# Hybrid stream step: the last unit's ScalarE stores go to SP, a head's keys are loaded and split apart from its queries, and one normalization is read four ticks later

## The chip, the cores and the metric

The kernel runs on one core of a Trainium2 chip. The metric is the time of one execution on the device in microseconds. An execution was recorded by the hardware profiler as well; its trace is what the text below quotes.

## The reference, cut to what matters

One layer handles 512 frames of a new stream (the prompt) and 64 frames of a running one (the samples), which has 512 cached frames:

```python
hn = rmsnorm(x, g_norm1);  proj = hn @ w_in          # 576 x 2048 @ 2048 x 6144
q, k, v, gb, gc, hc = split(proj)                    # 8 heads x 128; 3 x 1024 channels
q = rmsnorm(q, g_q);  k = rmsnorm(k, g_k)            # per head and frame
# stick-breaking attention, strictly causal: z = q k / sqrt(128)
# w[t,s] = sigmoid(z[t,s]) * prod over s<j<t of (1 - sigmoid(z[t,j]));  o_attn = w @ v
o_conv = gb * causal_conv3(gc * hc)
x = x + concat(rmsnorm(o_attn), rmsnorm(o_conv)) @ w_out
h2 = rmsnorm(x, g_norm2)
x = x + (silu(h2 @ w_gate) * (h2 @ w_up)) @ w_down   # 2048 -> 5632 -> 2048
```

The outputs are the new x of both streams, the new keys and values, and the convolution's states.

## The kernel before, in words

Frames lie in the columns, 576 of them in two halves of 288 (`HALVES`), the first 512 the prompt's. Products are exact to float32: each operand is split into a rounded high part and a low part (`split`, L228 the cast on ScalarE, L229 the difference on VectorE), and the products high x high, low x high and high x low are added. The large projections run as units of seven products each (`run`, line 405 holds their matmuls), whose weights and frames are prepared ahead (`prepare`).

**The order of the work.** TensorE's order is the order in which the code is written. Work that has to stand between other work is written as generators of a `Pipeline`: a `yield n` puts the rest n ticks later, and a tick is, in the output projection, three matmuls of 288 columns (`product`, L224). ScalarE, VectorE, GpSimd and SP are ordered by a scheduler until the last phase, the down projection; there all four follow the code as well. `tc.issue_after(x)` keeps what is issued inside it behind instruction x.

**Normalization.** When a half of a head's queries or keys is done, `a_done` scales it (L899), squares it, casts the squares on ScalarE (L904) and takes the low part on VectorE (L905). `normed` (L844) waits 20 ticks and then sums high and low part over the channels with two matmuls (`channel_sums`, L283 and L284) on TensorE.

**Attention.** The output projection of the convolution's half (`out_proj`, `pjo`) fills TensorE while the eight heads go by, one every 29 ticks (`PERIOD`). `attend(h)` writes one head: the scores of the key blocks 2 and 3, 1, and 0 (`scores`, L1173 and L1176), their softplus, the scores of the samples' queries against their 64 new keys and the cached ones (`zs`, L1204) and their softplus, cumulated over blocks into `sp`. Eleven ticks later come the sums over keys that the product over j needs, block by block: block 2, four ticks, block 1, four ticks, block 0. `weights(b)` masks a block (L1229), takes its exponential (L1231) and splits it into `ph` and `pl`. Then the output `po` is summed: L1280 and L1283. Between, `sample_weights` adds the sums of `sp` to the samples' scores (L1219 to L1222, from `sph` and `spl`).

The queries and keys of the next head come from DRAM: `load_qk` (L1033) loads all 576 columns of both into `qf` and `kf`, behind the scores of the samples, which read both. `split_qk` splits their first 512 columns into `qh`, `ql`, `kh`, `kl` behind `weights(2)`; the samples' sums are split into `sph`, `spl` behind `weights(1)`. The next head's first scores read all four parts.

**The end.** The last unit of the down projection finishes four blocks of the output. All others are transposed by VectorE in pieces and stored by SP with six small DMAs each (`store_blocks`, L1613 and L1615), for a block nine and then five ticks behind its sum. The four of the last unit are transposed by TensorE (`store_y`, L1644), copied by ScalarE (L1647 and L1653) and stored row-wise: for the first half of the frames one DMA of SP (L1656) and GpSimd's, for the second half one of SP (L1635), then one of 96 rows (prompt) and one of 32 rows (samples) on ScalarE (`put`, L1635 and L1637), and GpSimd's.

Every DMA that SP or ScalarE issues adds to one of eight counters, DMAHW0 to DMAHW7, when it has landed. The counters are dealt out in turn to the DMAs of both engines together, in the order of the program, and a DMA is issued only when the one before it on its counter has landed.

Of the kernel before, what the change touches and what calls it, by code (L numbers as in the profile page):

```python
# [10 lines left out]
F32 = mybir.dt.float32  # L11
F32R = mybir.dt.float32r
AF = mybir.ActivationFunctionType
# [3 lines left out]
P = 128  # L17
TP = 512
TS = 64
T = TP + TS  # L20
# [5 lines left out]
NH = 8  # L26
# [32 lines left out]
NA = len(HEADS_A)  # L59
# [43 lines left out]
def tile_hybrid_stream_step(  # L103
# [6 lines left out]
    nc = tc.nc  # L110
    mm = nc.tensor.matmul
# [23 lines left out]
    qk_dram = tc.dram_tile([NH, 2, P, T], F32, name="qk_dram")  # L135
# [20 lines left out]
    NU = len(gu)  # L156
# [70 lines left out]
    def split(hi, lo, src, lo_eng=None):  # L227
        cast = nc.scalar.copy(out=hi, in_=src)  # L228
        (lo_eng or nc.vector).tensor_tensor(out=lo, in0=src, in1=hi.bitcast(F32), op=ALU.subtract)  # L229
        return cast.ins  # L230
# [611 lines left out]
        return ((a, min(b, TP), 0),) + (((TP, b, 2),) if b > TP else ())  # L842

    def normed(n, h, c, a, b, s2, E):  # L844
        yield 12 if n == -2 else 20
        ms = ss = channel_sums(s2[:, 0], s2[:, 1], a, b, "ss")
        yt = hl_tile("yt")
        y, t = yt[:, :HALF], yt[:, HALF:]
        nc.scalar.activation(out=ms, in_=ss, func=AF.Identity, scale=1.0 / P, bias=epsc)
        nc.scalar.activation(out=y, in_=ms, func=AF.Ln)  # L850
        nc.scalar.activation(out=y, in_=y, func=AF.Exp, scale=-0.5)
        nc.scalar.activation(out=t, in_=y, func=AF.Square)
        nc.vector.scalar_tensor_tensor(out=t, in0=t, scalar=-0.5, in1=ms, op0=ALU.mult, op1=ALU.mult)
        nc.vector.scalar_tensor_tensor(out=t, in0=t, scalar=1.5, in1=y, op0=ALU.add, op1=ALU.mult)
        nc.vector.scalar_tensor_tensor(out=E[:, a:b], in0=E[:, a:b], scalar=col("gk") if c else gqs, in1=t,
                                       op0=ALU.mult, op1=ALU.mult)
        seen[n, c] = seen.get((n, c), 0) + 1
        if seen[n, c] == 2:
            nc.sync.dma_start(out=qk_dram[h, c], in_=E)
            if c:  # L860
                pipe.spawn((last_tokens if n == -2 else tokens)(E, kp[:, h, :], ks[:, h, :], None, 11 if n == -2 else 20))
# [152 lines left out]
    free.clear()  # L1014
    lpool.release()
    bpool = tc.alloc_tile_pool(name="bpool", bufs=1, reuse_waits="tile", side="left")
    qf, kf = (bpool.tile([P, T], F32, name=name) for name in ("qf", "kf"))
    qh, ql, kh, kl = (bpool.tile([P, TP], F32R, name=name) for name in ("qh", "ql", "kh", "kl"))
    cK = bpool.tile([P, 4, P], F32, name="cK")
    ws = bpool.tile([P, 320], F32, name="ws")  # L1020
# [10 lines left out]
    vz = bpool.tile([P, 2, P], F32R, name="vz")  # L1031

    def load_qk(h):  # L1033
        nc.sync.dma_start(out=qf, in_=qk_dram[h, 0])
        nc.sync.dma_start(out=kf, in_=qk_dram[h, 1])

    def split_qk():
        split(qh, ql, qf[:, :TP])
        split(kh, kl, kf[:, :TP])

    def load_cached_keys(h):
        nc.sync.dma_start(out=cK, in_=ck[:, h, :].rearrange("(i p) d -> p i d", p=P))
# [5 lines left out]
        nc.sync.dma_start(out=cV, in_=cv[:, h, :].rearrange("(i p) d -> p i d", p=P))  # L1048

    load_qk(0)  # L1050
    split_qk()
    load_cached_keys(0)
    fetch_v(0)
# [76 lines left out]
    def softplus(dst, ps, scratch):  # L1130
        nc.scalar.activation(out=scratch, in_=ps, func=AF.Abs)
        nc.scalar.activation(out=scratch, in_=scratch, func=AF.Exp, scale=-1.0)
        nc.scalar.activation(out=scratch, in_=scratch, func=AF.Ln, bias=1.0)
        nc.vector.scalar_tensor_tensor(out=dst, in0=ps, scalar=0.0, in1=scratch, op0=ALU.max, op1=ALU.add)

    kw = dict(start=False, skip_group_check=True)
    bt = {}
# [27 lines left out]
    def attend(h):  # L1165
# [12 lines left out]
        for b in (2, 1, 0):  # L1178
# [15 lines left out]
            if b == 1:  # L1194
                nc.gpsimd.tensor_tensor(out=pb[1][:, P:], in0=pb[1][:, P:], in1=pb[2], op=ALU.add)
                split(s0h, s0l, pb[1])
            yield 3 if b else 1
            if h == 0 and b == 1:
                keys_cached(0)

        zs = misc("zs")
        for n, b in enumerate((4, 3, 2, 1, 0)):
            lk = kf[:, T - P : T] if b == 4 else kcT[:, b * P : (b + 1) * P]
            mm(zs[:, b * TS : (b + 1) * TS], lk, qf[:, TP:T], start=(n == 0), stop=False, skip_group_check=True)  # L1204
        if h + 1 < NH:
            load_qk(h + 1)
        softplus(sp[:, :320], zs[:, :320], sp[:, :320])
        nc.gpsimd.tensor_tensor(out=sp[:, 256:320], in0=sp[:, 256:320], in1=s01, op=ALU.mult)
        sums = sp[:, 320:]
        nc.gpsimd.tensor_copy(sums[:, 192:256], sp[:, 256:320])  # L1210
        for b in (2, 1, 0):
            nc.gpsimd.tensor_tensor(out=sums[:, b * TS : (b + 1) * TS], in0=sums[:, (b + 1) * TS : (b + 2) * TS],
                                    in1=sp[:, (b + 1) * TS : (b + 2) * TS], op=ALU.add)
        yield 8
        if h == 0:
            split_v()
# [23 lines left out]
        mm(zb[2], trir, ph[2], stop=False, **kw)  # L1240
        mm(zb[2], trir, pl[2], stop=True, **kw)
        behind = weights(2)
        if h + 1 < NH:
            with tc.issue_after(behind):
                split_qk()
        yield 4
        mm(zb[1], trir, ph[1], stop=False, **kw)
        mm(zb[1], trir, pl[1], stop=False, **kw)
        mm(zb[1][:, P:], neg1r, s1h, stop=False, **kw)
        mm(zb[1][:, P:], neg1r, s1l, stop=True, **kw)  # L1250
        behind = weights(1)
        with tc.issue_after(behind):
            split(sph, spl, sp)
        yield 4
        mm(zb[0], trir, ph[0], stop=False, **kw)
        mm(zb[0], trir, pl[0], stop=False, **kw)
# [365 lines left out]
    def store_y(n, c, i):  # L1622
# [16 lines left out]
        def work():  # L1639
# [15 lines left out]
            if i == 0:  # L1655
                nc.sync.dma_start(out=yp[: 2 * P, cs].rearrange("(i p) c -> p i c", p=P), in_=ob)  # L1656
            else:
                put(f0, ob[:, 0, :])
                put(f0 + P, ob[:, 1, :], nc.scalar if n == NU - 1 else nc.sync)
            put(f0 + 2 * P, obs, nc.gpsimd if n == NU - 1 else nc.sync)  # L1660

        pipe.spawn(work())
# [82 lines left out]
```

## Time and profile before

| | us |
|---|---|
| median of 3 runs | 2339.37 (2337.11 to 2339.61) |
| the profiled execution | 2339.12 |
| its span, first to last instruction | 2337.4 |
| TensorE busy (matmuls) | 2316.1 |
| VectorE, ScalarE, GpSimd busy | 1954.1, 1221.6, 300.6 |

The 1.7 us between the profiled time and the span lie around the recorded instructions. Rows of a timeline give the start in us from the span's start, the duration, the engine (a name ending in q is its queue, where DMAs are issued and semaphores awaited), the line, the operation, output and input, and in brackets the idle time ahead with what ended it. TensorE's matmuls overlap: when nothing is awaited the next one starts before the last has ended, so the distance of two starts is the price of one. Rows of waits give the sum, the times and the longest.

### The profile page before, as it was taken

How to read it: one execution, taken by the hardware profiler on the slowest of the kernel's cores; microseconds unless marked ns; L12 is line 12 of the kernel's file. 1: busy time of each engine (PE TensorE's matmuls, PEld its weight loads, DVE VectorE, ACT ScalarE, POOL GpSimd, SP SyncE). 2: the span in 40 equal slices, each digit the busy share in tenths (PEclk: the TensorE clock that was granted, in tenths of full speed). 3: DMA queues.
4: the chain of work that ended last, by engine and by line, in shares of the span. 5: the costliest groups of instructions: out<-in, count | busy, mean ns of one | idle time of the engine just before them, and what ended most of it. 6: DMA issues, size and time to landing. Idle time of an engine off the chain costs nothing.

```text
span 2337.4 us, 43553 instructions
## 1 busy us (share of the span) xinstructions
PE 2316.1 (99%) x17432; PEld 2306.9 (99%) x17432; DVE 1954.1 (84%) x2871; ACT 1221.6 (52%) x2170; POOL 300.6 (13%) x374
## 2 busy tenths in 40 slices
PE   9999999999999999999999999999999999999997
PEld 9999999999999999999999999999999999999997
DVE  8889989897777898888888888888888778887896
ACT  8556656456877654444444444444444444444443
POOL 0211121110332320000000000000000002431222
PEclk9999999999999999999999999999999999999999
DMA  8434343546743454543444444444444936875653
GB/s 271 139 113 129 91 142 110 142 134 206 197 137 118 163 190 126 159 152 121 154 142 136 154 129 149 143 139 150 130 148 140 361 115 225 227 217 188 208 133 80
DMA packets 533771, 368.58 MB, mean 158 GB/s; under 512 B 70278, under 2 KB 518016, under 8 KB 533568
## 3 DMA queue, kind: packets, MB, share of 16 engines
q1 hardware_dynamic: 526752, 356.32, 48.7%
q0 software_dynamic: 6384, 9.21, 2.2%
q8 instruction: 136, 2.23, 0.4%
q14 instruction: 67, 0.55, 0.1%
q10 hardware_dynamic: 432, 0.27, 0.0%
HBM read 285.52 MB, written 80.23 MB: 156 GB/s over the span
## 4 chain that ended last, share of the span: by engine, by line
PE 92%; DVE 3%; ACT 3%; DMA 1%; issue 1%; POOL 0%; SPq 0%; POOLq 0%; DVEq 0%; ACTq 0%
PE psy L405 45%; PE psw L405 23%; PE psx L405 11%; PE pjo L224 6%; PE pj L691 1%; PE pjz L691 1%; DVE whl L229 1%; PE psv L405 1%; PE pjm L691 1%; DMA raw_a<-in_w_down_dram 0%; ACT ph L228 0%; PE psx L556 0%; ACT whi L176 0%; DMA raw_b<-in_w_down_dram 0%; PE z L1176 0%
## 5 line engine op out<-in xcount | busy, mean ns | idle before, releaser
L229 DVE TENSOR_TENSOR whl<-raw_a,whl 128x1024 fp32r<-128x1024 f32 (+4 forms) x384 | 432.2, 1126 | 54.8 <-ACT whl L228 53.4
L405 PE MATMUL psy<-t,whl 128*128 128x288 f32 x3000 | 447.0, 294 | 0.0
L228 ACT CAST whl<-raw_a 128x1024 fp32r<-128x1024 f32 (+4 forms) x384 | 360.1, 939 | 141.5 <-PE psx L405 46.7
L405 PE MATMUL psy<-h_s,whl 128*128 128x288 f32 x2766 | 416.5, 294 | 0.6 <-ACT part L428 0.6
L405 PEld LDWEIGHTS psy<-t,whl 128*128 128x128 f32 x3000 | 414.3, 188 | 0.0
L405 PE MATMUL psw<-t,whl 128*128 128x288 f32 x2688 | 388.9, 294 | 0.0
L405 PEld LDWEIGHTS psy<-h_s,whl 128*128 128x128 f32 x2766 | 383.1, 188 | 0.9 <-ACT part L428 0.8
L405 PEld LDWEIGHTS psw<-t,whl 128*128 128x128 f32 x2688 | 366.8, 188 | 0.0
L228 ACT CAST whl<-raw_b 128x1024 fp32r<-128x1024 f32 (+5 forms) x234 | 211.3, 905 | 208.1 <-issue 71.6
L229 DVE TENSOR_TENSOR whl<-raw_b,whl 128x1024 fp32r<-128x1024 f32 (+5 forms) x234 | 254.7, 1089 | 74.0 <-ACT whl L228 72.6
L428 ACT COPY part<-psy 128x288 f32<-128x288 f32 x309 | 123.1, 399 | 343.3 <-PE psy L405 340.9
L405 PE MATMUL psx<-h_s,whl 128*128 128x288 f32 x1164 | 170.2, 294 | 0.0
L405 PEld LDWEIGHTS psx<-h_s,whl 128*128 128x128 f32 x1164 | 159.6, 188 | 0.0
L228 ACT CAST whl<-s 128x1024 fp32r<-128x1024 f32 (+5 forms) x103 | 95.3, 925 | 122.6 <-PE psw L405 115.0
L405 PE MATMUL psy<-t12a,whl 128*128 128x288 f32 x1056 | 150.6, 295 | 0.4 <-ACT part L428 0.4
L405 PE MATMUL psw<-t34a,whl 128*128 128x288 f32 x1056 | 150.6, 295 | 0.0
L405 PEld LDWEIGHTS psy<-t12a,whl 128*128 128x128 f32 x1056 | 143.5, 188 | 0.9 <-ACT part L428 0.7
L405 PEld LDWEIGHTS psw<-t34a,whl 128*128 128x128 f32 x1056 | 143.3, 188 | 0.0
L1454 POOL DMA_DIRECT2D hid_dram<-form x7 | 5.2, 739 | 952.1 <-DVE form L229 944.9
L229 DVE TENSOR_TENSOR whl<-s,whl 128x1024 fp32r<-128x1024 f32 (+5 forms) x103 | 110.3, 1071 | 19.9 <-ACT whl L228 19.3
L224 PE MATMUL pjo<-mixc,whi 128*128 128x288 f32 x512 | 119.0, 300 | 0.0
L224 PE MATMUL pjo<-mixa,whi 128*128 128x288 f32 x512 | 102.8, 296 | 0.0
(565 smaller groups left out, 3920.6 us busy)
## 6 DMA issues: line engine op xcount, KB each, us to landing
hid_dram<-form SPq DMA_DIRECT2D x147, 288.0 KB
raw_a<-in_w_in_dram SPq DMA_DIRECT2D x22, 1024.0 KB
raw_b<-in_w_in_dram SPq DMA_DIRECT2D x22, 1024.0 KB
raw_b<-in_w_gate_dram SPq DMA_DIRECT2D x22, 1024.0 KB
raw_b<-in_w_up_dram SPq DMA_DIRECT2D x22, 1024.0 KB
raw_a<-in_w_gate_dram SPq DMA_DIRECT2D x22, 1024.0 KB
raw_a<-in_w_up_dram SPq DMA_DIRECT2D x22, 1024.0 KB
h_s<-hid_dram SPq DMA_DIRECT2D x10, 2016.0 KB
```

Of the source, the lines that this page charges most:

```text
L224: mm(ps, w_[:, k, csl], x_[:, a:b], start=(k == 0 and n == 0), stop=(k == nk - 1 and n == 2))
L228: cast = nc.scalar.copy(out=hi, in_=src)
L229: (lo_eng or nc.vector).tensor_tensor(out=lo, in0=src, in1=hi.bitcast(F32), op=ALU.subtract)
L405: mm(ps, whl[:, w_, j, :], x_, start=(start and j == 0 and q == 0), stop=(j == len(xs_) - 1 and q == 2), skip_group_check=True)
L428: nc.scalar.copy(out=t, in_=st["y"])
L691: mm(banks_[c][i], w3[:, kt % 8, c * P : (c + 1) * P], t[:, x_, :], start=(kt == 0 and n == 0), stop=(kt == KD - 1 and n == 2))
L1454: q.dma_start(out=hid_dram[fp][2 * n - 2 : 2 * n].rearrange("f p t -> p f t"), in_=t.bitcast(F32))
```

## The change

It has five parts. `normed` waits 24 ticks instead of 20 for one unit (the queries and keys of head 1, the fifth unit in `HEADS_A`). `qf` and `kf` hold only the 512 columns of the prompt; `load_qk` loads them, keys first, and now stands behind the scores of blocks 2 and 3. The 64 queries of the samples and the last 128 keys have their own tiles `qs` and `kz`, loaded by `load_samples` where `load_qk` stood. The keys are split behind the logarithm of the samples' softplus. Behind `weights(2)` the samples' sums are split first and then the next head's queries. And in the last unit the second half's DMAs of 96 and 32 rows are SP's.

```diff
--- before.py
+++ after.py
@@ -842,7 +842,7 @@
         return ((a, min(b, TP), 0),) + (((TP, b, 2),) if b > TP else ())
 
     def normed(n, h, c, a, b, s2, E):
-        yield 12 if n == -2 else 20
+        yield 12 if n == -2 else 24 if n == 4 - NA else 20
         ms = ss = channel_sums(s2[:, 0], s2[:, 1], a, b, "ss")
         yt = hl_tile("yt")
         y, t = yt[:, :HALF], yt[:, HALF:]
@@ -1014,7 +1014,8 @@
     free.clear()
     lpool.release()
     bpool = tc.alloc_tile_pool(name="bpool", bufs=1, reuse_waits="tile", side="left")
-    qf, kf = (bpool.tile([P, T], F32, name=name) for name in ("qf", "kf"))
+    qf, kf = (bpool.tile([P, TP], F32, name=name) for name in ("qf", "kf"))
+    qs, kz = (bpool.tile([P, n], F32, name=name) for name, n in (("qs", TS), ("kz", P)))
     qh, ql, kh, kl = (bpool.tile([P, TP], F32R, name=name) for name in ("qh", "ql", "kh", "kl"))
     cK = bpool.tile([P, 4, P], F32, name="cK")
     ws = bpool.tile([P, 320], F32, name="ws")
@@ -1031,12 +1032,16 @@
     vz = bpool.tile([P, 2, P], F32R, name="vz")
 
     def load_qk(h):
-        nc.sync.dma_start(out=qf, in_=qk_dram[h, 0])
-        nc.sync.dma_start(out=kf, in_=qk_dram[h, 1])
+        nc.sync.dma_start(out=kf, in_=qk_dram[h, 1, :, :TP])
+        nc.sync.dma_start(out=qf, in_=qk_dram[h, 0, :, :TP])
+
+    def load_samples(h):
+        nc.sync.dma_start(out=qs, in_=qk_dram[h, 0, :, TP:])
+        nc.sync.dma_start(out=kz, in_=qk_dram[h, 1, :, T - P :])
 
     def split_qk():
-        split(qh, ql, qf[:, :TP])
-        split(kh, kl, kf[:, :TP])
+        split(qh, ql, qf)
+        split(kh, kl, kf)
 
     def load_cached_keys(h):
         nc.sync.dma_start(out=cK, in_=ck[:, h, :].rearrange("(i p) d -> p i d", p=P))
@@ -1048,6 +1053,7 @@
         nc.sync.dma_start(out=cV, in_=cv[:, h, :].rearrange("(i p) d -> p i d", p=P))
 
     load_qk(0)
+    load_samples(0)
     split_qk()
     load_cached_keys(0)
     fetch_v(0)
@@ -1130,8 +1136,9 @@
     def softplus(dst, ps, scratch):
         nc.scalar.activation(out=scratch, in_=ps, func=AF.Abs)
         nc.scalar.activation(out=scratch, in_=scratch, func=AF.Exp, scale=-1.0)
-        nc.scalar.activation(out=scratch, in_=scratch, func=AF.Ln, bias=1.0)
+        log = nc.scalar.activation(out=scratch, in_=scratch, func=AF.Ln, bias=1.0)
         nc.vector.scalar_tensor_tensor(out=dst, in0=ps, scalar=0.0, in1=scratch, op0=ALU.max, op1=ALU.add)
+        return log.ins
 
     kw = dict(start=False, skip_group_check=True)
     bt = {}
@@ -1195,22 +1202,27 @@
                 nc.gpsimd.tensor_tensor(out=pb[1][:, P:], in0=pb[1][:, P:], in1=pb[2], op=ALU.add)
                 split(s0h, s0l, pb[1])
             yield 3 if b else 1
+            if b == 2 and h + 1 < NH:
+                load_qk(h + 1)
             if h == 0 and b == 1:
                 keys_cached(0)
 
         zs = misc("zs")
         for n, b in enumerate((4, 3, 2, 1, 0)):
-            lk = kf[:, T - P : T] if b == 4 else kcT[:, b * P : (b + 1) * P]
-            mm(zs[:, b * TS : (b + 1) * TS], lk, qf[:, TP:T], start=(n == 0), stop=False, skip_group_check=True)
+            lk = kz if b == 4 else kcT[:, b * P : (b + 1) * P]
+            mm(zs[:, b * TS : (b + 1) * TS], lk, qs, start=(n == 0), stop=False, skip_group_check=True)
         if h + 1 < NH:
-            load_qk(h + 1)
-        softplus(sp[:, :320], zs[:, :320], sp[:, :320])
+            load_samples(h + 1)
+        last = softplus(sp[:, :320], zs[:, :320], sp[:, :320])
         nc.gpsimd.tensor_tensor(out=sp[:, 256:320], in0=sp[:, 256:320], in1=s01, op=ALU.mult)
         sums = sp[:, 320:]
         nc.gpsimd.tensor_copy(sums[:, 192:256], sp[:, 256:320])
         for b in (2, 1, 0):
             nc.gpsimd.tensor_tensor(out=sums[:, b * TS : (b + 1) * TS], in0=sums[:, (b + 1) * TS : (b + 2) * TS],
                                     in1=sp[:, (b + 1) * TS : (b + 2) * TS], op=ALU.add)
+        if h + 1 < NH:
+            with tc.issue_after(last):
+                split(kh, kl, kf)
         yield 8
         if h == 0:
             split_v()
@@ -1240,17 +1252,16 @@
         mm(zb[2], trir, ph[2], stop=False, **kw)
         mm(zb[2], trir, pl[2], stop=True, **kw)
         behind = weights(2)
-        if h + 1 < NH:
-            with tc.issue_after(behind):
-                split_qk()
+        with tc.issue_after(behind):
+            split(sph, spl, sp)
+            if h + 1 < NH:
+                split(qh, ql, qf)
         yield 4
         mm(zb[1], trir, ph[1], stop=False, **kw)
         mm(zb[1], trir, pl[1], stop=False, **kw)
         mm(zb[1][:, P:], neg1r, s1h, stop=False, **kw)
         mm(zb[1][:, P:], neg1r, s1l, stop=True, **kw)
-        behind = weights(1)
-        with tc.issue_after(behind):
-            split(sph, spl, sp)
+        weights(1)
         yield 4
         mm(zb[0], trir, ph[0], stop=False, **kw)
         mm(zb[0], trir, pl[0], stop=False, **kw)
@@ -1656,7 +1667,7 @@
                 nc.sync.dma_start(out=yp[: 2 * P, cs].rearrange("(i p) c -> p i c", p=P), in_=ob)
             else:
                 put(f0, ob[:, 0, :])
-                put(f0 + P, ob[:, 1, :], nc.scalar if n == NU - 1 else nc.sync)
+                put(f0 + P, ob[:, 1, :])
             put(f0 + 2 * P, obs, nc.gpsimd if n == NU - 1 else nc.sync)
 
         pipe.spawn(work())
```

Line numbers behind the first part shift by 6 in the attention and by 11 from the stores on.

Three places of the order. First SP near the end of the program: the last stores of the blocks that VectorE transposes (`acc5` and the like show as `acc`), before.

```order
L1613 DMA out_dram<-acc_21201 32x9x32 [waits DMAHW3_49,DVE_49]
L1613 DMA out_dram<-acc_21201 32x9x32 [waits DMAHW5_49]
L1613 DMA out_dram<-acc_21201 32x9x32 [waits DMAHW7_49]
L1613 DMA out_dram<-acc_21201 32x9x32 [waits DMAHW1_49]
L1613 DMA out_dram<-acc_21202 32x7x32 [waits DMAHW3_49,DVE_49]
L1613 DMA out_dram<-acc_21202 32x7x32 [waits DMAHW4_49]
L1613 DMA out_dram<-acc_21202 32x7x32 [waits DMAHW5_49]
L1613 DMA out_dram<-acc_21202 32x7x32 [waits DMAHW6_49]
```

ScalarE at the end, before; `pot` has gone into its `acc` by the copies between.

```order
L1635 DMA out_dram<-acc_21048 96x128 [waits DMAHW4_49,Activation_49]
L1637 DMA out_dram<-acc_21048 32x128 [waits DMAHW6_49]
L1647 COPY acc_21047<-pot 128x256 [waits DVE_49,PE_49]
L1653 COPY acc_20721<-pot 32x128
L1647 COPY acc_21046<-pot 128x256 [waits DVE_49,PE_49]
L1653 COPY acc_20721<-pot 32x128
L1635 DMA out_dram<-acc_21046 96x128 [waits DMAHW0_49,Activation_49]
L1637 DMA out_dram<-acc_21046 32x128 [waits DMAHW2_49]
```

SP's counters run 3, 5, 7, 1, 3 and then 4: those left out, 4, 6, 0 and 2, are dealt to ScalarE's four DMAs. SP's second row of `acc_21202` waits on DMAHW4, which the DMA of 96 rows on ScalarE has last. With the change, SP's last rows:

```order
L1624 DMA out_dram<-acc_20739 32x9x32 [waits DMAHW4_49]
L1624 DMA out_dram<-acc_20739 32x9x32 [waits DMAHW5_49]
L1624 DMA out_dram<-acc_20739 32x9x32 [waits DMAHW6_49]
L1667 DMA out_dram<-acc_21063 128x2x128 [waits DMAHW7_49,Activation_49]
L1646 DMA out_dram<-acc_21066 128x128 [waits DMAHW0_49,Activation_49]
L1646 DMA out_dram<-acc_21066 96x128 [waits DMAHW1_49]
L1648 DMA out_dram<-acc_21066 32x128 [waits DMAHW2_49]
L1667 DMA out_dram<-acc_21065 128x2x128 [waits DMAHW3_49,Activation_49]
L1646 DMA out_dram<-acc_21064 128x128 [waits DMAHW4_49,Activation_49]
L1646 DMA out_dram<-acc_21064 96x128 [waits DMAHW5_49]
L1648 DMA out_dram<-acc_21064 32x128 [waits DMAHW6_49]
```

All eight counters follow each other on SP, ScalarE has no DMA there, and four more rows stand behind the blocks' stores, each behind the copy that it stores.

Second, ScalarE in the third head, from a cast of the values (`vtok`) to that of the samples' sums, before (`whi` is the output weights' high part; `hbl` holds block 1 and the sums, `hbe` block 2's high part).

```order
L228 CAST vz<-vtok 128x128
L1158 COPY kcT<-kc 128x512 [waits PE_49]
L176 CAST whi_7431<-raw_a 128x512 [waits DMAHW7_49,PE_49]
L176 CAST whi_7431<-raw_a 128x512 x3
L1231 ACTIVATE pr_6701<-z_7273 128x384 [waits DVE_49,PE_49]
L228 CAST hbe<-pr_6701 128x256 [waits Activation_49]
L228 CAST qh<-qf 128x512 [waits DMAHW2_49]
L228 CAST kh<-kf 128x512 [waits DMAHW3_49]
L1231 ACTIVATE hbl<-z_7309 128x384 [waits DVE_49]
L228 CAST ph_6704<-hbl 128x384 [waits Activation_49]
L228 CAST sph<-hbl 128x576 [waits Pool_49]
```

And with the change:

```order
L228 CAST vz<-vtok 128x128
L228 CAST kh<-kf 128x512 [waits DMAHW5_49]
L1165 COPY kcT<-kc 128x512 [waits PE_49]
L176 CAST whi_7443<-raw_a 128x512 [waits DMAHW2_49,PE_49]
L176 CAST whi_7443<-raw_a 128x512 x3
L1243 ACTIVATE pr_6703<-z_7281 128x384 [waits DVE_49,PE_49]
L228 CAST hbe<-pr_6703 128x256 [waits Activation_49]
L228 CAST sph<-hbl 128x576 [waits Pool_49]
L228 CAST qh<-qf 128x512 [waits DMAHW6_49]
L1243 ACTIVATE hbl<-z_7319 128x384 [waits DVE_49]
L228 CAST ph_6706<-hbl 128x384 [waits Activation_49]
```

The cast of the keys has moved up, ahead of the copy of the cached keys, and the cast of the sums stands ahead of that of the queries, behind block 2's cast.

Third, VectorE in the same head, before, from the second mask of block 2 on (`x` and `pjo` are the output projection's drain; `z_7309` is block 1, `z_7342` block 0).

```order
L1229 SCALAR_TENSOR_TENSOR z_7273<-z_7273,mneg 128x128 [waits DVE_49]
L177 TENSOR_TENSOR wlo_7432<-raw_a,whi_7431 128x512 [waits Activation_49] x2
L229 TENSOR_TENSOR hbe<-pr_6701,hbe 128x256 [waits Activation_49]
L229 TENSOR_TENSOR ql<-qf,qh 128x512 [waits DMAHW2_49,Activation_49]
L229 TENSOR_TENSOR kl<-kf,kh 128x512 [waits DMAHW3_49,Activation_49]
L1229 SCALAR_TENSOR_TENSOR z_7309<-z_7309,mneg 128x128 [waits PE_49]
L1104 TENSOR_TENSOR x_3_6917<-pjo,accc 128x288 [waits PE_49]
L1229 SCALAR_TENSOR_TENSOR z_7342<-z_7342,mneg 128x128 [waits PE_49]
L229 TENSOR_TENSOR pl_6705<-hbl,ph_6704 128x384 [waits Activation_49]
L229 TENSOR_TENSOR spl<-hbl,sph 128x576 [waits Activation_49]
```

And with the change, from the keys' low part on (`z_7281` is block 2, `z_7319` block 1):

```order
L229 TENSOR_TENSOR kl<-kf,kh 128x512 [waits DMAHW5_49,Activation_49]
L1110 TENSOR_TENSOR x_2_6741<-pjo,accc 128x288 [waits PE_49]
L177 TENSOR_TENSOR wlo_7444<-raw_a,whi_7443 128x512 [waits DMAHW2_49,Activation_49]
L1241 SCALAR_TENSOR_TENSOR z_7281<-z_7281,mneg 128x128 [waits PE_49]
L177 TENSOR_TENSOR wlo_7444<-raw_a,whi_7443 128x512 [waits Activation_49]
L1241 SCALAR_TENSOR_TENSOR z_7281<-z_7281,mneg 128x128 [waits DVE_49]
L177 TENSOR_TENSOR wlo_7444<-raw_a,whi_7443 128x512 [waits Activation_49]
L1241 SCALAR_TENSOR_TENSOR z_7319<-z_7319,mneg 128x128 [waits PE_49]
L177 TENSOR_TENSOR wlo_7444<-raw_a,whi_7443 128x512 [waits Activation_49]
L229 TENSOR_TENSOR hbe<-pr_6703,hbe 128x256 [waits Activation_49]
L229 TENSOR_TENSOR spl<-hbl,sph 128x576 [waits Activation_49]
L229 TENSOR_TENSOR ql<-qf,qh 128x512 [waits DMAHW6_49,Activation_49]
```

The keys' low part has moved up ahead of the weights' low parts, a mask of block 1 stands ahead of `hbe`, and `spl` and `ql` follow `hbe`. The next rows are `pl` of block 1 and only then the drain of the output projection, which stood ahead of both.

## The prediction

> **What bounds the kernel now.** I read the busy shares first, then the waits of the engine that is busiest, then the end of the program.
>
> ```profile
> PE 2316.1 (99%) x17432; PEld 2306.9 (99%) x17432; DVE 1954.1 (84%) x2871; ACT 1221.6 (52%) x2170; POOL 300.6 (13%) x374
> ```
>
> TensorE is busy for 99% of the span, so a change that leaves TensorE's work alone can only win what TensorE waits, and what lies behind its last matmul. In the view of waits, TensorE's rows from 600 to 760 us, the attention stage, are these two (us in all, times, longest):
>
> ```profile
> PE zs L1220 <- DVE spl L229: 1.6, 4, 0.6
> PE zs L1219 <- ACT sph L228: 0.3, 1, 0.3
> ```
>
> The change touches both, and one wait of 0.7 us in the projections (below). The rows undercount, since a matmul that waited is not overlapped with the one before it.
>
> The other place is the end. The waits of SP's own queue from 2300 us on, and its issues there (start, duration, line, count):
>
> ```profile
> SPq L1613 <- DMA out_dram<-acc: 11.2, 2, 11.0
> ```
>
> ```profile
> 2308.44 18.29 SPq L1613 DMA_DIRECT2D out_dram<-acc  x12
> 2326.78 1.13 SPq L1615 DMA_DIRECT2D out_dram<-acc  x2
> 2328.01 1.97 SPq L1613 DMA_DIRECT2D out_dram<-acc  x4
> ...
> 2334.76 0.42 SPq L1635 DMA_DIRECT2D out_dram<-acc  x1
> ```
>
> SP issues stores to the very end. Four issues take 1.97 us, about 0.48 each, but a group of twelve took 18.29: one of them waited 11.0 us for another DMA. Three issues follow that wait in the group (3 x 0.45 back from 2326.73), so the hole is about 2314.4 to 2325.4. ScalarE and GpSimd at the same time:
>
> ```profile
> 2323.40 0.37 ACT L1647 COPY acc<-pot 128x256 f32<-128x256 f32 x1 [2.69 <-PE pot L1644]
> ...
> 2323.80 0.34 ACTq L1635 DMA_DIRECT2D out_dram<-acc  x1
> ...
> 2325.14 0.36 ACT L1647 COPY acc<-pot 128x256 f32<-128x256 f32 x1
> ```
>
> ```profile
> DMA to landing us min/median/max: 1.7/2.3/2.8
> ```
>
> ```profile
> L1741 POOLq EVENT_SEMAPHORE  x4: 17/17/17, 2336.7 to 2337.3; - x4
> L1741 POOLq DRAIN  x3: 40/93/3136, 2326.1 to 2337.1; - x3
> ```
>
> ScalarE's first store goes out at 2323.80. The landing row (of the stores of L1635, measured on GpSimd's) begins at 1.7 us: 2323.80 + 1.7 = 2325.5, which is when SP moves again. The issue rows shown with the change give the reason: SP's row behind the hole waits on counter DMAHW4, and the last DMA before it on that counter is ScalarE's first store, which stands ahead of SP's row in the program although its data come only with ScalarE's copy, at 2323.77. SP stands still for a store that isn't its own.
>
> **The tail.** The change puts those four stores behind SP's others, so SP runs through. From 2314.4 us, at the durations above: three issues left of the group (1.4), two of L1615 with their gap (1.2), four of L1613 (2.0), two (1.2), four (2.0) end at about 2322.2, and the first store of the last unit (0.5) at 2322.7. The next needs ScalarE's copy, 2323.40 + 0.37 = 2323.77; three issues of 0.5 end at 2325.3, one more at 2325.8, and the last three, whose copy ends at 2325.14 + 0.36 = 2325.50, at about 2327.2. Four issues are new on SP, 4 x 0.5 = 2.0 us, and they are in this count. Before, the last issue ended at 2335.18, 2.2 us before the span's end; so SP's path ends at 2329.4. GpSimd then is the later one: its drain of 3136 ns from 2326.1 lasts to 2329.2, and the program's close, 2336.7 to 2337.4, adds 0.7: 2329.9. ScalarE's copies wait for TensorE and move little. **Tail: 2329.9 - 2337.4 = -7.5 us.** Bounds: -8.0 (SP's path alone, 2329.4) and +2.0 (the hole stays and four issues are added); I take -7.5 because the issue time of one engine and the restart of the other meet within 0.1 us.
>
> **The normalization.**
>
> ```profile
> 176.78 0.29 PE L283 MATMUL ss<-s,oner 128*128 128x288 f32 x1
> 177.80 0.40 PE L284 MATMUL ss<-s,oner 128*128 128x288 f32 x1 [0.72 <-DVE s L905]
> 178.04 1.35 PE L405 MATMUL psy<-t12a,whl 128*128 128x288 f32 x9
> ```
>
> ```profile
> 177.30 0.45 DVE L905 TENSOR_TENSOR s<-psx,s 128x288 fp32r<-128x288 f32 x1
> ```
>
> Nine matmuls of 288 columns take 1.35 with 0.29 for the last, so they follow each other every 0.13 us; these two stand 1.02 apart: 0.9 lost. The data are there at 177.75. Four ticks are twelve such matmuls, 12 x 0.13 = 1.6 us: the pair would start at 178.4, behind its data. **-0.9 us**; bounds 0 and -0.9 (the other three halves of this unit never waited).
>
> **The attention.** The products with the samples' sums in the first head, and in the third:
>
> ```profile
> 601.38 0.31 PE L1219 MATMUL zs<-sph,trir 128*128 128x320 f32 x1
> 601.53 0.31 PE L1220 MATMUL zs<-spl,trir 128*128 128x320 f32 x1
> ```
>
> ```profile
> 642.92 0.41 PE L1219 MATMUL zs<-sph,trir 128*128 128x320 f32 x1 [0.32 <-ACT sph L228]
> 643.71 0.41 PE L1220 MATMUL zs<-spl,trir 128*128 128x320 f32 x1 [0.38 <-DVE spl L229]
> 643.96 0.28 PE L1221 MATMUL zs<-sph,neg1r 128*128 128x256 f32 x1
> ```
>
> At 601 us, without a wait, the second product follows after 0.15; here after 0.79, the third after another 0.25, and the first came late by 0.32: 1.2 us lost, of which the rows book 0.32 + 0.38 = 0.70. The 1.9 us that the waits' two rows book in all are so worth 1.9 x 1.2 / 0.7 = 3.3. Casting the sums earlier removes them. But in the third head VectorE is a chain without gaps, and the change puts two things into it.
>
> ```profile
> 634.00:642.00 8.00, 7.16 (x17) 1.00 0.53 97
> ```
>
> ```profile
> 639.25 0.41 DVE L229 TENSOR_TENSOR hbe<-pr,hbe 128x256 fp32r<-128x256 f32 x1
> 639.72 0.69 DVE L229 TENSOR_TENSOR ql<-qf,qh 128x512 fp32r<-128x512 f32 x1
> 640.33 0.69 DVE L229 TENSOR_TENSOR kl<-kf,kh 128x512 fp32r<-128x512 f32 x1
> ...
> 642.90 0.76 DVE L229 TENSOR_TENSOR spl<-hbl,sph 128x576 fp32r<-128x576 f32 x1
> ```
>
> ```profile
> 640.19 0.61 PE L1283 MATMUL po<-hbe,vz 128*128 128x256 f32 x3
> ...
> 641.29 0.28 PE L1176 MATMUL z<-ql,kh 128*128 128x256 f32 x1
> ```
>
> VectorE is busy for 7.16 of these 8 us (the window's row: length, busy, instructions). So there is little slack to fill: `kl`, 0.6 from start to start like `ql` (639.72 to 640.33), now comes ahead of this whole stretch, so the masks, the exponential and `hbe` of block 2 come 0.6 later; and one more mask is ordered ahead of `hbe`, 0.2. Its low part, which ended at 639.25 + 0.41 = 639.66, ends at 640.5 to 640.7, and the third of the three products from 640.19, at about 640.5, waits for it: 0.3 with the restart. Then `spl` (0.76 long, 0.66 to the next start) stands ahead of `ql`: `ql`, which began at 639.72, begins at 641.3 and ends at 641.95, while the next head's scores want it at 641.29, or 641.6 behind the first wait: **a new wait of 0.4 us**. This head wins only 1.2 - 0.3 - 0.4 = 0.5. The new wait should come in the other heads too, 0.4 x 7 = 2.8, also where there was none to remove. The drain of the output product `x` moves behind `spl`, `ql` and `pl`, by about 1.2 us in this head; I price that as one such wait over all heads, 1.1. Sum: -3.3 + 2.8 + 0.3 + 1.1 = **+0.9 us**. Bounds: -3.3 (none of the new waits) and, at 0.60 + 0.66 = 1.26 us of VectorE ahead of `ql` with no slack left, 7 x 1.26 - 3.3 = +5.5. In this head `ql` ended 0.9 us before it was wanted (639.72 + 0.69 = 640.41, 641.29), a slack that eats most of it, so I stay low.
>
> The loads: per head four DMAs instead of two, two more issues of 0.4 us on an SP that has free time here:
>
> ```profile
> 651.46 0.38 SPq L1035 DMA_DIRECT2D kf<-qk_dram  x1
> ```
>
> ```profile
> 654.87 0.47 ACT L1133 ACTIVATE hbl<-hbl 128x320 f32<-128x320 f32 x1
> ...
> 660.18 0.62 ACT L228 CAST kh<-kf 128x512 fp32r<-128x512 f32 x1
> ```
>
> Keys issued at 651.46 were cast 8.7 us later without a wait. In the change they are issued behind the scores of 641 us and cast behind the logarithm of 654.87: 13 us, so this costs nothing unless the issue is held up (last rival).
>
> **Sum** against the profiled execution (2339.1 us, of which 2337.4 are the span; 0.3 below the median of 2339.4): 2339.1 - 7.5 - 0.9 + 0.9 = **2331.6 us**.
>
> **The rivals.**
> - *No new waits in attention.* If `ql` and the drain fit into slack that I don't see, -3.3 instead of +0.9: 2327.4. For it: only four of eight heads are booked with a wait for `spl`, so the others have slack. Against it: the chain worked out above.
> - *The new waits at full price*, +5.5: 2336.2. For it: VectorE is busy 84% of the span and SP, ScalarE and TensorE all hang on its order here.
> - *The hole is SP's own.* If SP stood for a store of its own, ScalarE's were bystanders and the move only adds four issues: 2339.1 + 2.0 - 0.9 + 0.9 = 2341.1, slower than before. It decides if the first store on SP behind the hole still waits past 2323 us. Against it: the meeting at 2325.4, and the counter. The Trainium skill, page "DMA: Bandwidth & Descriptors", section "Issuing engines are not separate DMA queues", speaks for this rival: DMAs of all engines run on the same sixteen DMA engines, and spreading the issues saves only the issuing time. By that rule gathering them on SP could only cost; the 11 us hole is more than the rule has room for, since a store of one engine held an issue of another.
> - *Keys late.* If the early load stood behind SP's wait for a weight buffer, the key cast, now ahead in two in-order queues, would hold ScalarE and VectorE, and all behind them.
>
> ```profile
> SPq L184 <- DVE wlo L177: 67.4, 7, 17.4
> ```
>
>   That wait is 9.6 us in the mean. It decides once keys land over 13 us after the scores; 2 us in each of 7 heads would give 2339.1 - 8.4 + 14 = 2344.7. Against it: in the order of the change the keys' issue comes ahead of the weights' one in most heads.
>
> **Chances.** Forecast as worked out 0.60 (2329 to 2334.5); no new waits 0.19; new waits at full price 0.11; SP's own hole 0.06; keys late 0.04. The range takes in the first three: 2327.0 to 2336.5. A measurement of this kernel can tell about 0.2%, 4.7 us, from no change, so faster means below 2334.7: the first two cases, 0.79. Same: full price and SP's own hole, 0.17. Slower: 0.04.
>
> **What would show it.** Tail: no 11 us row for SP, its last issue near 2327 us on the old time scale, GpSimd's drain ahead of the close. Normalization: the row of L284 gone. Attention: the rows of `zs` gone, and rows for `z` from `ql` (some 0.4 each) and for `po` from `hbe`. The prediction is wrong if SP still waits there, or if the new waits come to more than 4 us.

## The result, and the profile after

The changed kernel takes 2331.43 us (median of 10 runs, 2330.24 to 2333.72), the kernel before 2339.18 (10 runs, 2337.11 to 2340.81). The ratio is 0.9968 with a 95% interval of 0.9959 to 0.9978: 7.75 us less, 0.33%, clear of the 0.2%. The forecast was 2331.6.

**The tail.** SP's issues in the changed kernel, from the group of twelve that took 18.29 us before:

```profile
2309.28 7.46 SPq L1624 DMA_DIRECT2D out_dram<-acc  x12
2316.78 1.13 SPq L1626 DMA_DIRECT2D out_dram<-acc  x2
2318.01 1.88 SPq L1624 DMA_DIRECT2D out_dram<-acc  x4
2319.93 1.13 SPq L1626 DMA_DIRECT2D out_dram<-acc  x2
2321.16 1.91 SPq L1624 DMA_DIRECT2D out_dram<-acc  x4
2323.17 0.40 SPq L1667 DMA_DIRECT2D out_dram<-acc  x1
2324.69 0.83 SPq L1646 DMA_DIRECT2D out_dram<-acc  x2
2325.57 0.42 SPq L1648 DMA_DIRECT2D out_dram<-acc  x1
...
2327.55 0.42 SPq L1648 DMA_DIRECT2D out_dram<-acc  x1
```

The twelve take 7.46 us, and nothing else in the list changed its pace; the gap from 2323.6 to 2324.7 is the wait for ScalarE's copy, which the waits of SP's queue have as 1.2 us. SP's row of 11.2 us for a DMA is gone, and this one has come:

```profile
SPq L1646 <- ACT acc L1664: 1.2, 1, 1.2
```

**TensorE.** Its waits from 560 to 870 us, the attention with the whole output projection:

```profile
PE z L1183 <- DVE ql L229: 1.2, 4, 0.4
PE po L1294 <- ACT ph L228: 0.7, 1, 0.7
PE zs L1213 <- ACT kcT L1165: 0.3, 1, 0.3
PE po L1294 <- DVE hbe L229: 0.2, 1, 0.2
```

The two rows of `zs` on the sums, 1.9 us, are gone, and 2.1 us in rows for `ql`, `ph` and `hbe` have come, beside one of 0.3 for `kcT`. The wait of the normalization's sums is gone as well; its two matmuls now follow each other in 0.13 us:

```profile
178.47 0.29 PE L283 MATMUL ss<-s,oner 128*128 128x288 f32 x1
178.60 0.30 PE L284 MATMUL ss<-s,oner 128*128 128x288 f32 x1
```

**Where the time went**, from the two traces. The marks are starts of matmuls: the first and the last of the output projection (`pjo`) and the last of `pot`, the end of TensorE's work.

| us | before | after | difference |
|---|---|---|---|
| start to first `pjo` | 569.1 | 568.3 | -0.9 |
| first to last `pjo` (attention) | 284.7 | 287.1 | +2.4 |
| last `pjo` to last `pot` | 1470.4 | 1469.8 | -0.6 |
| last `pot` to the end | 13.2 | 4.9 | -8.3 |
| span | 2337.4 | 2330.1 | -7.4 |

The first stretch contains reads of the input whose wait differs from run to run (TensorE waited 4.0 us there in one trace, 4.6 in the other). Traces of the same code differ by 2.2 us in the first stretch (567.9 to 570.1 in the four with the normalization of before), by 1.2 in the third (1469.5 to 1470.7 in all thirteen), and by 1.5 in the second (284.3 to 285.8 in the five with the attention of before; 287.1 and 288.2 in the two with the change's). The last one hardly differs: 13.1 to 13.4 in four traces with ScalarE's stores, 4.9 in all nine with SP's.

The attention's +2.4 us can be split further, since both traces have the same matmuls in the same order there. For each one I took the distance of its start from the start ahead of it, after minus before, and added these up by what it computes (us; the last column is the forecast):

| matmuls | after minus before | forecast |
|---|---|---|
| products with the samples' sums (`zs` from `sph`, `spl`) | -3.7 | -3.3 |
| next head's scores (`z`) | +3.1 | +2.8 |
| `po` of block 2, with `hbe` | +0.8 | +0.3 |
| `po` of blocks 1 and 0, with `ph` and `pl` | +0.8 | |
| `pjo`, much of it right behind the above | +0.7 | |
| `zs` from `kcT` and from `ws` | +0.7 | |
| drain of `x` | no wait of its own | +1.1 |
| sum | +2.4 | +0.9 |

### The profile page after: what moved, and what is told of

Its sections match the earlier page's. It is cut to its first block, busy times and chain, and to the rows that moved or that the text cites. A ratio compares the mean times of both kernels' runs of the same rounds, so it can differ in the third digit from the quotient of the medians.

```text
span 2330.1 us, 43590 instructions
## 1 busy us (share of the span) xinstructions
PE 2317.3 (99%) x17432; PEld 2307.4 (99%) x17432; DVE 1951.7 (84%) x2871; ACT 1222.4 (52%) x2170; POOL 300.9 (13%) x374
## 4 chain that ended last, share of the span: by engine, by line
PE 92%; ACT 3%; DVE 2%; POOL 1%; DMA 1%; issue 1%; POOLq 0%; SPq 0%; ACTq 0%; DVEq 0%
PE psy L405 47%; PE psw L405 24%; PE psx L405 12%; PE pjo L224 5%; PE pj L691 1%; PE pjz L691 1%; PE psv L405 1%; PE pjm L691 1%; ACT ph L228 1%; PE psx L556 0%; DVE wlo L177 0%; DVE pl L229 0%; ACT pr L1243 0%; DVE hbe L229 0%; ACT hbe L228 0%
```

## The experiments

Times are medians; each ratio is against the kernel before on the same chip, with its 95% interval.

**1. The stores alone.**

```diff
-                put(f0 + P, ob[:, 1, :], nc.scalar if n == NU - 1 else nc.sync)
+                put(f0 + P, ob[:, 1, :])
```

> Of the change only the last unit's stores: the four DMAs of ScalarE go to SP, nothing else. My theory (SP stood 11.0 us on counter DMAHW4 for ScalarE's first store): the hole goes, SP's last issue ends near 2327 us, the whole is 7.5 to 8.2 us faster, about 2331.4. Rival (the hole is SP's own, spreading issues only saves issuing time): four more issues of 0.5 us, 2 us slower, 2341.

Measured 2331.56 us against 2339.26, ratio 0.9964 (0.9952 to 0.9976). SP's queue at the end:

```profile
2309.55 7.45 SPq L1613 DMA_DIRECT2D out_dram<-acc  x12
```

7.7 us from one line: by the medians the stores carry the whole gain of the change. The rival of 2341 falls.

**2. The four ticks alone.**

```diff
-        yield 12 if n == -2 else 20
+        yield 12 if n == -2 else 24 if n == 4 - NA else 20
```

> Of the change only the four ticks in the normalization of head 1. Theory: one wait of 0.9 us goes, 2338.3. Between the two traces the stretch from the first normalization to the output projection became 1.7 us shorter; if the ticks did all of that, 2337.5; if the other 0.8 is chance from run to run, 0.9 it is. Rival: nothing, the wait comes back elsewhere, 2339.2.

Measured 2337.73 us, ratio 0.9994 (0.9985 to 1.0003). The median is 1.5 us lower, and the interval holds both 0.9 and nothing. TensorE's waits from 100 to 560 us, before, and then here:

```profile
PE ss L284 <- DVE s L905: 0.7, 1, 0.7
PE psy L405 <- ACT part L428: 0.4, 1, 0.4
```

```profile
PE psy L405 <- ACT part L428: 1.1, 1, 1.1
```

The row of L284 is gone, as it should; the second row varies by itself. In the other traces of code with 20 ticks it is 0.5 or missing. The row of L284 varies too: with 20 ticks it is 0.7 in three traces and 0.2 in experiment 4's. By the medians the size of this term lies between nothing and 3.5 us. The traces give it closer: from the first normalization to the first `pjo` the four with 20 ticks take 440.5 to 441.9 us, 441.5 in the mean, and the nine with 24 ticks 440.1 to 441.4, 440.7 in the mean. That is 0.9 less, though any two single traces can differ by more.

**3. The attention alone.** The diff of the change without its first and last part.

> Of the change only the attention: keys loaded and split early, samples' sums split ahead of the queries. Prediction's term +0.9 us (2340.1); by the two traces' stage times +2.4 us (2341.6), with waits of z on ql. Rival (no new waits): 3.3 us faster, 2335.9.

Measured 2340.92 us against 2339.26, ratio 1.0006 (0.9997 to 1.0014): 1.7 us more by the medians, no gain. The interval includes 1, no change, but the rival (3.3 us faster, a ratio of 0.9986) lies outside it. The waits are those of the whole change:

```profile
PE z L1183 <- DVE ql L229: 1.2, 4, 0.4
PE po L1294 <- ACT ph L228: 0.7, 1, 0.7
PE po L1294 <- DVE hbe L229: 0.2, 1, 0.2
```

By the medians the attention's part so gives back what the ticks won, and neither is clear of noise by itself. Its stretch is 288.2 us here.

**4. ScalarE keeps its stores and issues them later.** This tells the counter from the issuing engine.

```diff
-                put(f0 + P, ob[:, 1, :], nc.scalar if n == NU - 1 else nc.sync)
+                if n < NU - 1:
+                    put(f0 + P, ob[:, 1, :])
             put(f0 + 2 * P, obs, nc.gpsimd if n == NU - 1 else nc.sync)
+            if i and n == NU - 1:
+                yield 40
+                put(f0 + P, ob[:, 1, :], nc.scalar)
```

> The kernel before, ScalarE keeps its four stores but issues them behind all its copies, 1.9 us later for the first. In the order SP's third row of acc_21202 now waits on DMAHW5, which the first of them has last; so the counters are still dealt among SP's rows. Theory: the hole stays and ends where ScalarE's first store lands, near 2327.4 instead of 2325.4, with one issue more done ahead of it: 1.5 us slower, about 2340.7. Rival (the hole is SP's own): SP's rows are the same, the hole ends at 2325.4 as before, no difference.

Measured 2339.51 us, ratio 1.0001 (0.9992 to 1.0009): no difference by the medians, where 1.5 us more was expected; the interval holds both. The trace decides, and it shows the hole moved by one row. SP before (two parts of its queue: up to the hole, and behind it):

```profile
2314.12 0.32 SPq L1613 DMA_DIRECT2D out_dram<-acc  x1
```

```profile
2325.43 1.31 SPq L1613 DMA_DIRECT2D out_dram<-acc  x3
```

and here, with ScalarE's first store:

```profile
2312.99 0.80 SPq L1613 DMA_DIRECT2D out_dram<-acc  x2
```

```profile
2325.12 0.81 SPq L1613 DMA_DIRECT2D out_dram<-acc  x2
```

```profile
2323.53 0.33 ACTq L1635 DMA_DIRECT2D out_dram<-acc  x1
```

Before, one of the four stores of `acc_21202` went ahead of the hole and three behind it, the first of these waiting on DMAHW4. Here two went ahead, and the third, which waits on DMAHW5, was held, because DMAHW5 is what ScalarE's first store has here. It was released 1.6 us behind that store's issue, as before (2323.80 to 2325.43). SP's own rows are the same in both. The semaphores recorded in the two traces say the same: the held row waits for the very one to which ScalarE's first store adds, and this is another one here than before. Which row is held follows the counter that ScalarE's store has: the mechanism is shown. The size was wrong since ScalarE's store went out only 0.8 us later against TensorE's end (0.4 us behind the start of the last `pot` matmul, 2323.2; before, 0.4 ahead of it, 2324.2), not 1.9, and one issue more was done ahead of the hole: 0.8 - 0.45 leaves some 0.35. From the last `pot` to the end the trace has 13.4 us, against 13.2 before.

This also corrects a sentence in the description of the kernel before. The counters aren't dealt in the order of the code: the stores moved to the end of the code, and their counters still lie among SP's rows. They are dealt in a common order of both engines that is fixed when the program is built, and which has ScalarE's stores far earlier against SP's than they run.

**5. Stores and ticks, the attention as before.** Experiments 1 and 2 together.

> The stores on SP and the four ticks, the attention as before the change. If the attention's part costs 1.7 us (measured alone), this is faster than the whole change by that: 2329.8. Rival (the attention's part is chance): 2331.4, as the whole change.

Measured 2329.66 us (2329.25 to 2330.47), ratio 0.9962 (0.9949 to 0.9974). The two parts alone give a median 1.8 us lower than the whole change, as experiment 3 says; the two ratios' intervals overlap. The stretch of the attention is 284.3 us, and the waits on the sums are back:

```profile
PE zs L1220 <- DVE spl L229: 1.3, 4, 0.4
PE zs L1219 <- ACT sph L228: 0.3, 1, 0.3
```

**6. The whole change, queries split ahead of the sums.**

```diff
         with tc.issue_after(behind):
-            split(sph, spl, sp)
             if h + 1 < NH:
                 split(qh, ql, qf)
+            split(sph, spl, sp)
```

> The whole change, but behind block 2 the queries are split ahead of the samples' sums. Theory (ql stands behind spl's 0.66 us): ql of the third head ends near 641.4 instead of 642.07, all of the z waits on ql go, the sums at 642.1 are still ahead of the 643.4 when they are used; 1.2 us booked, about 1.7 with restarts: 2329.7. Rival (ql is late because of the keys ahead of block 2): the waits stay at 0.3 or more, 2331.4.

Measured 2331.21 us, ratio 0.9967 (0.9955 to 0.9979): no gain. The rows of `z` on `ql` are gone, as expected, and others stand in their place:

```profile
PE po L1294 <- ACT ph L228: 0.7, 1, 0.7
PE po L1294 <- DVE hbe L229: 0.5, 2, 0.3
PE zs L1308 <- ACT ws L1237: 0.3, 1, 0.3
```

The booked waits fell from 2.4 to 1.5 us, the stretch from 287.1 to 286.5. So `ql` behind `spl` was one wait of several, and taking it away didn't take away the loss.

**7. The sums third.** Stores and ticks as changed, the attention of before, with one move:

```diff
-        if h + 1 < NH:
-            with tc.issue_after(behind):
+        with tc.issue_after(behind):
+            if h + 1 < NH:
                 split_qk()
+            split(sph, spl, sp)
         yield 4
...
-        behind = weights(1)
-        with tc.issue_after(behind):
-            split(sph, spl, sp)
+        weights(1)
```

> Stores and ticks as changed; of the attention only one thing is changed against before: the samples' sums are split behind block 2, after the queries and the keys, with no early keys and no other loads. Theory (nothing then stands ahead of ql, and spl ends near 641.7 where it is used at 642.4): the waits of zs go without new ones, up to 3.3 us less than the kernel with stores and ticks alone, 2326.5 to 2328. Rival (VectorE is full, any order gives a wait elsewhere): no gain, 2329.8.

Measured 2329.35 us, ratio 0.9960 (0.9947 to 0.9972). Neither row of `zs`, none of `z` or `hbe`; but

```profile
PE po L1282 <- ACT ph L228: 1.0, 2, 0.7
PE po L1282 <- DVE pl L229: 0.2, 1, 0.2
```

The stretch is 283.5 us, 0.8 less than in experiment 5, and the median 0.3 less, both within what runs of one code differ by. Both views were half right: the waits on the sums go at no cost to the queries, and most of what they were worth comes back one consumer later, at the output of the blocks whose probabilities are now split behind the sums.

**8. The first head's new loads behind its values**, on experiment 6:

```diff
     load_qk(0)
-    load_samples(0)
     split_qk()
     load_cached_keys(0)
     fetch_v(0)
+    load_samples(0)
```

> As the kernel with the queries first, and the first head's two new loads for the samples issued behind the values instead of ahead of them. Theory: the wait of zs on kcT in the first head, 0.3 booked and 0.5 lost in the changed kernel, goes: 0.5 us less, 2329.2. Rival (kcT is late for another reason): the wait stays, 2329.7.

Measured 2331.58 us, ratio 0.9970 (0.9958 to 0.9981). No gain, and the theory falls: experiment 6 has the changed loads and no row of `zs` on `kcT`, while experiment 1, with the loads of before, has one:

```profile
PE zs L1204 <- ACT kcT L1158: 0.6, 1, 0.6
```

That wait comes and goes between runs; the change isn't its cause.

**9. The change with the key split put back.** Early loads kept; behind block 2 the queries, the keys, then the sums.

```diff
-        if h + 1 < NH:
-            with tc.issue_after(last):
-                split(kh, kl, kf)
...
         with tc.issue_after(behind):
-            split(sph, spl, sp)
             if h + 1 < NH:
-                split(qh, ql, qf)
+                split_qk()
+            split(sph, spl, sp)
```

> The whole change with its loads, but the keys are split behind block 2 again, after the queries and ahead of the samples' sums; so the early loads are kept and the early key split is undone. Theory (the cost of the attention's part is the key split ahead of block 2): the waits of po on hbe and of z on ql go, and the time is that of the kernel with the sums third (2329.35) plus the first head's wait on kcT (0.5): 2329.9. Rival (the loads cost it): 2331.4, as the change.

Measured 2328.54 us (2327.84 to 2329.96), ratio 0.9956 (0.9943 to 0.9968), the lowest median of all, 2.9 us below the change's, though the intervals of the two ratios overlap. Two neighbours say what did it. Experiment 6 differs from this kernel in the early key split alone: its median is 2.7 us higher, each of its six runs (from 2330.29) is above each of the five here, and its stretch of the attention is 286.5 us against 284.2. The two ran on different chips, on which the kernel before differed by 0.4 us. So in this order the early key split costs some 2.3 us. Experiment 7 differs in the loads alone, and its median isn't lower (2329.35): the loads are free. The waits here are those of experiment 7:

```profile
PE po L1291 <- ACT ph L228: 1.1, 2, 0.7
PE po L1291 <- DVE pl L229: 0.2, 1, 0.2
```

**10. Keys early, sums as before.**

```diff
-        with tc.issue_after(behind):
-            split(sph, spl, sp)
-            if h + 1 < NH:
+        if h + 1 < NH:
+            with tc.issue_after(behind):
                 split(qh, ql, qf)
...
-        weights(1)
+        behind = weights(1)
+        with tc.issue_after(behind):
+            split(sph, spl, sp)
```

> The whole change, but the samples' sums are split behind block 1 as before; keys loaded and split early. Theory (the early key split costs by itself): zs waits on spl stay, 2 us or more, po waits on hbe are added, and the time is above the change's: 2332 to 2333, against 2329.7 of the kernel with stores and ticks alone. Rival (the sums' new place costs, the keys are free): no more than 2329.7.

Measured 2330.32 us (2330.00 to 2330.92), ratio 0.9963 (0.9950 to 0.9975): above experiment 5 by 0.7, but not above the whole change. The ratios of the two, 0.9963 and 0.9962, don't tell them apart. The stretch is 286.0 us against 284.3.

```profile
PE zs L1232 <- DVE spl L229: 1.5, 3, 0.7
PE zs L1231 <- ACT sph L228: 0.9, 2, 0.7
```

No row for `hbe` is booked, but the waits on the sums grew from 1.6 (experiment 5) to 2.4 us: with the keys ahead of block 2 all behind it comes later, the sums too. The trace points to a cost of the early split with this order as well, less than I had said; the times don't show it.

**11. The sums' low part on GpSimd**, on experiment 7: `split(sph, spl, sp, nc.gpsimd)`.

> The kernel with the sums third, with the low part of the sums taken by GpSimd instead of VectorE: 0.66 us less on VectorE in each head, ahead of block 1's mask. Theory (VectorE's order is what TensorE waits for): the waits of po on ph and pl shrink, 0.5 to 1.5 us less than 2329.35 if GpSimd is done within the 1.5 us from the cast to its use; it has taken 0.8 to 1.1 us for half as many columns, so 1.6 to 2.2 are needed, and a wait of zs on GpSimd in some heads is likely: 2328 to 2330.

Measured 2329.79 us, ratio 0.9959 (0.9945 to 0.9973): no gain over experiment 7. No row waits for GpSimd, but

```profile
PE z L1176 <- DVE kl L229: 0.8, 2, 0.6
PE po L1282 <- DVE pl L229: 0.7, 2, 0.5
PE zs L1204 <- ACT kcT L1158: 0.6, 1, 0.6
PE po L1282 <- ACT ph L228: 0.3, 1, 0.3
```

VectorE has one operation less in each head, and its rows `kl` and `pl` are waited for more. The trace shows a part of the reason: three of the sixteen `pl` of 384 columns began while GpSimd took `spl` (1.4 to 1.8 us each) and needed 606 to 982 ns, the other thirteen 543 to 560. Whether that is all of it stays open.

## Why the prediction was right

The time, 2331.6 against 2331.43, and the direction were right, and the reason given for it, SP held for a store of ScalarE, was confirmed by experiments 1 and 4. That the time was met within 0.2 us is luck. By the steps:

- **The tail**: -7.5 predicted, -7.7 alone (medians), -8.3 in the traces. The hole and its cause are as predicted. Mis-sized was GpSimd's drain, the path that I let set the end. It took 3136 ns before, which I carried over; this is its row now:

```profile
L1752 POOLq DRAIN  x3: 40/93/2256, 2326.3 to 2329.8; - x3
```

  Its 2256 ns last from 2326.3 to 2328.6 and end ahead of SP, whose last issue ends at 2327.97 and the program 2.1 us later. SP sets the end, close to the 2.2 us that the prediction had for it (2.1 in all nine traces with SP's stores). The tail of -8.3 is nearly the bound of -8.0 that it gave for SP's path alone. The drain is short because it waits for GpSimd's last store: in all thirteen traces it ends 0.4 us behind the landing of that store. From issue to landing GpSimd's two stores of L1637 took, before, and with the change (now L1648):

```profile
DMA to landing us min/median/max: 1.7/2.2/2.7
```

```profile
DMA to landing us min/median/max: 1.8/1.8/1.9
```

  The last store is the 2.7 before and the 1.9 after. Why it landed later before isn't shown; experiment 3, with ScalarE's stores as before, has 1.9.
- **The normalization**: -0.9 predicted, the wait gone, and 0.9 less in the mean of the traces (experiment 2).
- **The attention**: +0.9 predicted; +1.7 alone, +2.4 by the traces, inside the bounds of -3.3 and +5.5. The sign was right. In the third head the order and the times of VectorE came as worked out. The predicted waits for `hbe` and `ql` there, and what came (the second fence is VectorE):

```profile
640.86 0.38 PE L1294 MATMUL po<-hbe,vz 128*128 128x256 f32 x1 [0.20 <-DVE hbe L229]
...
642.13 0.38 PE L1183 MATMUL z<-ql,kh 128*128 128x256 f32 x1 [0.24 <-DVE ql L229]
...
643.37 0.31 PE L1231 MATMUL zs<-sph,trir 128*128 128x320 f32 x1
643.51 0.31 PE L1232 MATMUL zs<-spl,trir 128*128 128x320 f32 x1
```

```profile
636.42 0.68 DVE L229 TENSOR_TENSOR kl<-kf,kh 128x512 fp32r<-128x512 f32 x1
...
640.39 0.41 DVE L229 TENSOR_TENSOR hbe<-pr,hbe 128x256 fp32r<-128x256 f32 x1
640.72 0.75 DVE L229 TENSOR_TENSOR spl<-hbl,sph 128x576 fp32r<-128x576 f32 x1
641.39 0.68 DVE L229 TENSOR_TENSOR ql<-qf,qh 128x512 fp32r<-128x512 f32 x1
```

  `hbe` ends at 640.80 (640.5 to 640.7 was worked out), `ql` at 642.07 (641.95), and the two products with the sums follow each other without a wait. But what these waits cost TensorE was mis-sized. The old waits I had priced by the distances of starts, 1.2 us for 0.7 booked; the new ones I priced at little more than the wait itself. By the distances the head lost 0.9 us from the first `po` of block 2 to the `pjo` behind `hbe` (0.3 was forecast) and 0.5 at the scores (0.4), and won back 1.2 at the sums: 0.2 us lost in all, where 0.5 was to be won. Over all heads the scores' wait came near its price, +3.1 for 2.8, although it is booked in four heads and not in seven; missing in the sum are 0.5 us for `hbe` and 1.4 for `pjo`, `kcT` and `ws`, for which it had nothing (the row for `kcT` comes and goes, experiment 8). The drain that I priced at 1.1 us is no wait of its own, but in the last head 0.7 us are booked where the product with `ph` of block 0 waits for its cast.

```profile
750.18 0.72 PE L1294 MATMUL po<-ph,hbe 128*128 128x512 f32 x2 [0.69 <-ACT ph L228]
```

  Before, the trace has no wait there; it has one at the sums just ahead of it, booked with 0.25 us.

So the right total hides two terms that were off by 0.8 us (the tail) and 1.5 us (the attention, by the traces), in opposite directions, and the kernel's runs differ by as much.

The rivals: *SP's own hole* falls by experiment 1. With it falls what I drew from the Trainium skill, page "DMA: Bandwidth & Descriptors", section "Issuing engines are not separate DMA queues": no run here tests whether the DMA engines are shared, but by that rule only issuing time was at stake, 2.0 us, and the stores were worth 7.7, since the issues of two engines were tied to each other. *No new waits* and *full price* both missed: the new waits came and cost 6.1 us by the distances (2.4 + 3.7), where full price was 8.8 (7 x 1.26). *Keys late* falls by the trace: ScalarE waits for a key load once, 0.2 us in the first head, and the seven early loads are issued from 9.8 to 15.0 us ahead of their cast. Experiment 9 fits: the loads cost nothing, and the early split of the keys does.

## What to carry to other kernels

When an issue queue stands still for a DMA, ask whose DMA it is: its counter may belong to a store of another engine whose data come much later, and moving that store to the same queue costs the time of its issue, here half a microsecond, and saves the wait. Where TensorE waits for an operand of an engine that is nearly full, moving that operand ahead mostly renames the wait: of the 3.3 us estimated for the sums (3.7 by the distances), every order tried gave back most at the next consumers, and the orders that put more work ahead of the chain (the keys) were no faster or lost. A new wait has to be priced as an old one is, with the time that the matmuls behind it lose. Of this change the stores are worth having, the early loads are free, and the early key split is better left out: 2328.54 us.

## What the runs showed of the hardware

- A store by ScalarE released SP's next issue on the same counter 1.6 us behind its own issue, twice (2323.80 to 2325.43, 2323.53 to 2325.12); in this program DMAs of SP and ScalarE share eight counters, so two queues that issue independently can hold each other.
- GpSimd's last drain took 3136 ns in one trace and 2256 in another with the same DMAs ahead of it, and ended 0.4 us behind the landing of GpSimd's last store in all thirteen: its length follows that landing, which took 1.9 to 2.7 us from the issue, and can't be taken over as a constant.
- Runs of the same code differ by up to 1.4 us in the stretch up to the output projection (440.5 to 441.9 us from the first normalization to the first `pjo` in four traces with identical code there), which is the size of the two smaller terms of this change.
